# High and low parts of the stationary weight panels interleaved word by word in one tile, on a hybrid recurrent and attention step

## The chip, the cores and the metric

The kernel runs on one core of one Trainium2 chip, as one launch. The metric is device time in microseconds (us) from launch to end; lower is better. Durations of single instructions and waits are read from one profiled execution of the kernel before. Engines are named as the profile names them: PE (matrix multiplication), PEld (the loads of PE's stationary operand, which run beside PE's matmuls), DVE (vector engine), ACT (scalar engine), POOL (GpSimd), SP (issues most DMAs).

## The reference

One layer of a streaming encoder is computed for a prompt of 1024 rows and a sample of 64 rows, 1088 rows together, each 1024 wide, all in float32:

```
xn = rms_norm(x, g_pre)
z = xn @ w_in                                   # 1024 x 8208
xa, ga, q, k, v, gb, fl, ma, mb = split(z)      # branch A, branch B, merge gates
ua = causal_conv(xa);  ya = rg_lru(ua) * silu(ga)          # recurrence over the rows
yb = attention(q, k, v, cumsum(log_sigmoid(fl + b_f))) * silu(gb)   # 16 heads of 64
u = stack([ya, yb]) @ w_branch                   # two 1024 x 1024 products
mix = sum(sigmoid([ma, mb]) * u) @ w_o
h = x + rms_norm(mix, g_post)
h = h + rms_norm(sigmoid(h @ w_ple_gate) * (pe @ w_ple_proj), g_ple)
```

Keys, values, forget logarithms and the last states of the recurrence are outputs too. What the change touches are the products with `w_in` (all columns but those of v and the forget logits) and with `w_branch`.

## The kernel before, in words

**Three matmuls for one product.** Every float32 operand is split into a high part, which the ACT engine writes by a rounding copy (`copy_act`, line 83, output type fp32r), and a low part, which DVE writes as the difference of the value and its high part (`sub`, line 86). A product is then three matmuls that add into one PSUM bank: high by high, high by low, low by high (`three`, lines 163 to 166). Each matmul is preceded by its own load of the stationary operand, a block of 128 x 128 words. So there are as many loads as matmuls, 10117 of each.

**Panels.** In most of the kernel the stationary operand is a block of weights, and the activations, held transposed in SBUF as `xh`, `xl` (or `yah`, `yal`, `ybh`, `ybl`), stream past it. A panel is 128 columns of a weight matrix: 1024 x 128 words, kept as 8 blocks `wh[:, k, :]` (high) and 8 blocks `wl[:, k, :]` (low), each tile 128 partitions x 1024 words, in the pool `wpool` with two buffers per name. `load_panel` brings the raw words into `w_raw` by DMA; `split_next`, `book_split` or `weights_of`, by stage, has ACT and DVE split them; `panel_steps` (lines 185 to 195) or `dense` and `held` multiply: for each of three chunks of the 1088 rows (368, 368 and 352 of them) and each of 8 blocks k, three matmuls.

**Quads.** From about 147 to 413 us twelve pairs of panels go through a Strassen-like scheme (`split_pair` and `seven`, lines 626 to 925): seven products instead of eight, of half-size blocks, each over two half-banks of 272 rows. Weights for it are the raw halves (`a11`, `a12`, `a22`) and sums of them (`s1` to `s4`). `split` inside `split_pair` puts their high and low parts into `wpool` tiles of 8 blocks and into tiles `wh8`, `wl8` (8 blocks) and `wh4`, `wl4` (4 blocks) of a second pool. `product` (line 785) issues for each block and each of the three parts two matmuls of 272 rows (line 792), each with its own load.

**What sets the order.** PE's order is written out by hand. In the stages of attention and of the recurrence the orders of ACT and DVE are too, by planners with fixed costs; in the quads a scheduler orders ACT, DVE, POOL and SP by when operands and tiles come free. A tile is free for its next use when the last reader of its old content is done.

**Stages.** In order of time: values (v) and the transposition of x, 0 to 123 us, weights here being the moving operand; two panels; the quads; attention, with panels as fillers between its steps, 437 to 857 us; branch A with its recurrence, 857 to 1024; the product of ya, to 1119; of yb, to 1214; then `w_o` and the last gate, to the end, where weights are again the moving operand (`wqh`, `wql`).

**Where a high and a low part are not panels.** `wvh`, `wvl`, `wqh`, `wql`, `wph`, `wpl`, the gate blocks `g_h`, `g_l` of the recurrence, and one panel of the product of ya that is split into a free tile of `yb` (line 274's argument `rooms`) have tiles of their own.

Of the kernel before, what the change touches and what calls it, by code (L numbers as in the profile page):

```python
# [8 lines left out]
F32R = mybir.dt.float32r  # L9
# [4 lines left out]
P = 128  # L14
D = 1024
KT = D // P
# [50 lines left out]
def hybrid_step(tc, a, o):  # L67
# [4 lines left out]
    def sb(name, bufs=1, side=None):  # L72
        kw = {"side": side} if side else {}
        return Pool(tc, name=name, bufs=bufs, reuse_waits="tile", **kw)
# [4 lines left out]
    def f(ap):  # L79
        return ap.bitcast(F32)  # L80

    def copy_act(out, in_, scale=1.0):
        return act.activation(out=out, in_=in_, func=AF.Copy, scale=scale)  # L83

    def sub(eng, out, in0, in1):
        return eng.tensor_tensor(out=out, in0=in0, in1=in1, op=ALU.subtract)  # L86
# [121 lines left out]
    wpool = sb("wpool", bufs=2)  # L208
# [2 lines left out]
    raw_pair = w_raw.rearrange("p (k n) -> p k n", k=KT)  # L211
    raw_half = [w_raw[:, i * KT * P:(i + 1) * KT * P] for i in range(2)]

    def panels(src):
        return [src[..., i * P:(i + 1) * P] for i in range(2)]

# [32 lines left out]
    def look_ahead():  # L249

        while len(ahead) < 2:
            if held_back[0] and len(gates) <= n_gates - PLAIN // 2:
                return
            if not (gates or later):
                return
            src, tags = (gates or later)[0]
            if any(not e[3] and max(len(tags), e[4]) > 1 for e in ahead):
                return
            (gates or later).popleft()
            if len(tags) > 1:  # L260
                dst = raw_pair
                raws_ = panels(raw_pair)
            else:
                dst = raw_half[n_single[0] % 2].rearrange("p (k n) -> p k n", k=KT)
                raws_ = [dst]
                n_single[0] += 1
            load_panel(dst, src, tc.keep_in_program_order)
            for tag, raw in zip(tags, raws_):
                ahead.append([tag if isinstance(tag, tuple) else ("r", tag), raw, None, False, len(tags)])

    def split_next(eng, rooms=None):
        if ahead and ahead[0][2] is None:
            raw = ahead[0][1]
            wh, wl = rooms or [wpool.tile([P, KT, P], F32R, name=n) for n in ("wh", "wl")]
            copy_act(wh[:, :, :], raw)
            sub(eng, wl[:, :, :], raw, f(wh[:, :, :]))
            ahead[0][2:4] = (wh, wl), True

    def panel(eng=None):

        look_ahead()
        if not ahead:
            return None
        split_next(eng or dve)
        tag, _, w, *_ = ahead.popleft()
        look_ahead()
        split_next(eng or dve)
        look_ahead()
        return tag, w
# [152 lines left out]
    def weights(k, c):  # L442
        c0, w = VCH[c]
        return wvh[:, k, c0:c0 + w], wvl[:, k, c0:c0 + w]
# [51 lines left out]
    for name in ("conv_w", "conv_b", "b_rg_a", "b_rg_x", "a_param", "state_h", "state_conv"):  # L496
        n = a[name].shape[0]
# [76 lines left out]
    for b in range(2, NBLK + 1):  # L574
        _, n, t0 = x_src[b]
        for c, (_, w) in enumerate(VCH):
            acc = p1v.tile([P, 512], F32, name="vacc", tag="vacc")
            if b < NBLK:
                for k in range(KT):
                    turn_next(b, c, k)  # L580
                    wh, wl = weights(k, c)
# [24 lines left out]
        if b == NBLK - 2:  # L606
            look_ahead()
            split_next(dve)
        elif b == NBLK - 1:
            plain_1 = panel()  # L610
# [11 lines left out]
    def load_pair(i):  # L622
        raw = sp_.tile([P, KT, 2 * P], F32, name="wraw", tag="wraw", bufs=1)[:, :, :] if i % 2 else raw_pair
        src = quads[i][0]
        for dst, s in zip([raw] if len(src) == 1 else panels(raw), src):
            load_panel(dst, s)
        return panels(raw)

    def split_pair(i, raws_, got):

        a1, a2 = raws_
        a11, a12, a21, a22 = a1[:, :4, :], a1[:, 4:, :], a2[:, :4, :], a2[:, 4:, :]

        def split(pl, names, parts, bufs):
            n = 4 * len(names)
            sfx = "" if pl is wpool else str(n)
            wh = pl.tile([P, n, P], F32R, name="wh" + sfx, tag="wh" + sfx, bufs=bufs)
            wl = pl.tile([P, n, P], F32R, name="wl" + sfx, tag="wl" + sfx, bufs=bufs)
            for i_, x in enumerate(parts):
                ks_ = slice(4 * i_, 4 * i_ + x.shape[1])  # L640
                copy_act(wh[:, ks_, :], x)
                sub(dve, wl[:, ks_, :], x, f(wh[:, ks_, :]))
            for i_, name in enumerate(names):
                got[name] = wh[:, 4 * i_:4 * i_ + 4, :], wl[:, 4 * i_:4 * i_ + 4, :]

        s1, s2, s4 = (sp_.tile([P, 4, P], F32, name=f"s{j}")[:, :, :] for j in (1, 2, 4))
        pool.tensor_tensor(out=s1, in0=a21, in1=a22, op=ALU.add)
        sub(pool, s2, s1, a11)
        sub(pool, a21, a11, a21)
        sub(pool, s4, a12, s2)  # L650
        yield
        split(wpool, ("a11", "a12"), [a1[:, :, :]], 2)
        yield
        split(sp_, ("s2", "s3"), [s2, a21], 1)
        yield
        split(wpool, ("s1", "a22"), [s1, a22], 2)
        yield
        split(sp_, ("s4",), [s4], 1)
        yield
# [322 lines left out]
    def book(engine, at, ns, do=None):  # L982

        busy = booked[engine]
        while busy and busy[0][1] < now[0] - 20000.0:
            busy.pop(0)
        i = 0
        while i < len(busy) and busy[i][0] < at + ns:
            at = max(at, busy[i][1])
            i += 1  # L990
        busy.insert(i, (at, at + ns))
        if do is not None:
            serial[0] += 1
            heapq.heappush(agenda, (at, serial[0], do))
        return at + ns + HOP
# [23 lines left out]
    def book_split():  # L1019

        if ahead and ahead[0][2] is None:
            e = ahead[0]
            raw = e[1]
            wh = wpool.tile([P, KT, P], F32R, name="wh")
            wl = wpool.tile([P, KT, P], F32R, name="wl")
            e[2] = wh, wl

            def low():
                sub(dve, wl[:, :, :], raw, f(wh[:, :, :]))
                e[3] = True  # L1030
                look_ahead()

            at = book("A", now[0] + 5000.0, A_W, lambda: copy_act(wh[:, :, :], raw))
            book("D", at, D_W, low)
# [339 lines left out]
    def step(engine, ns, do, r=(), w=(), lag=0.0, after=(), table=None, bank=0, ahead_of=0.0, frees=False):  # L1374
        i = len(todo)
        deps = set(after)
        for x in (*r, *w):
            deps |= {written[x]} if x in written else set()
        for x in w:
            deps |= read_by.get(x, set())  # L1380
        for x in w:
            written[x], read_by[x] = i, set()
        for x in r:
            if x not in w:
                read_by.setdefault(x, set()).add(i)
        todo.append((engine, ns, do, deps, lag, table, bank, ahead_of, frees))
        return i
# [68 lines left out]
    def weights_of(tag, lag=0.0):  # L1456

        n = len(w_at)
        after = [last_use[n - 2]] if n > 1 else []
        if lag:  # L1460
            after.append(step("S", 0.0, lambda: None, after=w_at[-1:], lag=lag))
        got = {}

        def hi():
            look_ahead()
            e = next(x for x in ahead if x[0] == tag)
            got["e"] = e
            if e[2] is None:
                e[2] = tuple(wpool.tile([P, KT, P], F32R, name=x) for x in ("wh", "wl"))
                copy_act(e[2][0][:, :, :], e[1])  # L1470
                got["new"] = True

        def lo():
            e = got["e"]
            if "new" in got:
                sub(dve, e[2][1][:, :, :], e[1], f(e[2][0][:, :, :]))
            e[3] = True
            look_ahead()

        i = step("A", A_W if n else 0.0, hi, after=after)  # L1480
        w_at.append(step("D", D_W if n else 0.0, lo, after=[i]))

        def take():
            assert ahead[0][0] == tag
            got["w"] = ahead.popleft()[2]
            look_ahead()

        return got, take
# [349 lines left out]
    for of in range(KT):  # L1838
# [11 lines left out]
        else:  # L1850
            tag, w = panel()
# [42 lines left out]
    for of in range(KT):  # L1894
# [12 lines left out]
        tag, w = panel()  # L1907
# [77 lines left out]
    for q in range(NQ):  # L1985
# [7 lines left out]
        wh, wl = wo[q]  # L1993
        qc = slice(q * QW, (q + 1) * QW)
        for b in range(NBLK + 1):
            _, n, t0 = x_src[b]
# [97 lines left out]
    n = x_src[b][1]  # L2094
# [69 lines left out]
```

## Time and profile before

| | us |
|---|---|
| median of 3 runs (1456.34 to 1457.87) | 1456.99 |
| the profiled execution's own time | 1456.83 |
| its span, first to last instruction | 1454.9 |
| PE busy | 1438.2 |
| PEld busy | 1417.9 |
| DVE busy | 867.1 |
| ACT busy | 718.4 |
| POOL busy | 275.7 |

Between the span and the execution's own time lie 1.9 us. Matmuls are pipelined and their recorded durations overlap, so the pace of matmuls is read from the distance of their starts, not from their durations. The loads of the stationary operand overlap likewise.

### The profile page before, as it was taken

Reading aid. Unit: us, or ns where it says so; the run is one execution under the profiler, and the core shown is the slowest. Engines: PE = TensorE matmul, PEld = TensorE weight load, DVE = VectorE, ACT = ScalarE, POOL = GpSimd, SP = SyncE. Lnnn points to the kernel's source line nnn. Section 1 sums busy time; section 2 is a strip of 40 time slices with the busy share of each in tenths; the row PEclk is TensorE's granted clock in tenths of the full one; section 3 lists DMA queues with packets and bytes.
Section 4 is the critical chain, followed back from the end, with each engine's and each line's share of the span. In section 5 each row is a group of like instructions: output and inputs, shape, how many; then the busy total and the mean of one; then the engine's idle time right before and its main releaser. Section 6 shows DMA issues by size and latency. Waiting matters only on the chain.

```text
span 1454.9 us, 26374 instructions
## 1 busy us (share of the span) xinstructions
PE 1438.2 (99%) x10117; PEld 1417.9 (97%) x10117; DVE 867.1 (60%) x1571; ACT 718.4 (49%) x1389; POOL 275.7 (19%) x363
## 2 busy tenths in 40 slices
PE   8999999999999999999999999999999999999997
PEld 8999999999999999999999999999999999999997
DVE  5554765665425666666556557799745555248634
ACT  5424444443225666565555557869543333334633
POOL 0003333413222332333223210000122000000001
PEclk9999999999999999999999999999999999999999
DMA  5366455664276665636646242121486444214111
GB/s 206 114 137 99 143 161 179 176 186 120 82 215 160 118 148 146 139 105 158 103 114 159 51 100 51 51 58 33 162 294 212 153 150 137 74 46 146 51 45 44
DMA packets 140793, 182.85 MB, mean 126 GB/s; under 512 B 22788, under 2 KB 111404, under 8 KB 140668
## 3 DMA queue, kind: packets, MB, share of 16 engines
q1 hardware_dynamic: 122684, 154.90, 40.5%
q10 hardware_dynamic: 17680, 25.64, 5.0%
q8 instruction: 80, 1.31, 0.4%
q0 software_dynamic: 304, 0.62, 0.1%
q14 instruction: 45, 0.37, 0.1%
HBM read 122.65 MB, written 58.46 MB: 124 GB/s over the span
## 4 chain that ended last, share of the span: by engine, by line
PE 94%; DVE 2%; DMA 2%; ACT 1%; issue 1%; SPq 0%; ACTq 0%; DVEq 0%
PE quad L792 16%; PE acc L164 16%; PE acc L165 16%; PE acc L166 16%; PE tp L1145 4%; PE pv L1173 3%; PE pv L1175 3%; PE s L1123 2%; PE s L1124 2%; PE vacc L164 1%; PE vacc L166 1%; PE vacc L165 1%; PE vacc L457 1%; DMA out_v_prompt<-v_sb 1%; DMA wv_raw<-in_w_in 1%; PE tp L1953 1%
## 5 line engine op out<-in xcount | busy, mean ns | idle before, releaser
L164 PE MATMUL acc<-xh,wh 128*128 128x368 f32 (+1 forms) x768 | 252.7, 329 | 0.0
L165 PE MATMUL acc<-xl,wh 128*128 128x368 f32 (+1 forms) x768 | 251.5, 327 | 0.0
L166 PE MATMUL acc<-xh,wl 128*128 128x368 f32 (+1 forms) x768 | 251.0, 327 | 0.0
L164 PEld LDWEIGHTS acc<-xh,wh 128*128 128x128 f32 x768 | 144.6, 188 | 0.7
L165 PEld LDWEIGHTS acc<-xl,wh 128*128 128x128 f32 x768 | 144.7, 188 | 0.6
L166 PEld LDWEIGHTS acc<-xh,wl 128*128 128x128 f32 x768 | 144.7, 188 | 0.0
L1103 DVE CUSTOM_DVE_ANT_0 s<-s,mask 128x1024 f32<-128x1024 f32 (+7 forms) x128 | 95.5, 767 | 25.6 <-PE s L1124 25.3
L86 DVE TENSOR_TENSOR wl<-w_raw,wh 128x1024 fp32r<-128x1024 f32 (+1 forms) x65 | 74.7, 1149 | 60.4 <-ACT wh L83 55.4
L83 ACT ACTIVATE wh<-w_raw 128x1024 fp32r<-128x1024 f32 (+1 forms) x65 | 63.3, 975 | 76.1 <-PE acc L165 31.1
L1108 POOL TENSOR_SCALAR pb<-pb,sm 128x896 f32<-128x896 f32 (+1 forms) x64 | 61.6, 962 | 204.7 <-DVE sm L1107 183.9
L86 DVE TENSOR_TENSOR tl<-tp,th 128x512 fp32r<-128x512 f32 x96 | 65.8, 689 | 37.6 <-ACT th L83 37.5
L792 PE MATMUL quad<-xh,wh 128*128 128x272 f32 x384 | 80.7, 291 | 0.0
L792 PE MATMUL quad<-xl,wh 128*128 128x272 f32 x384 | 79.5, 288 | 0.0
L792 PE MATMUL quad<-xh,wl 128*128 128x272 f32 x384 | 79.4, 288 | 0.0
L1105 ACT ACTIVATE pb<-s,nm 128x896 f32<-128x896 f32 (+1 forms) x64 | 61.1, 954 | 33.3 <-DVE nm L1103 26.8
L83 ACT ACTIVATE th<-tp 128x512 fp32r<-128x512 f32 x96 | 56.9, 596 | 41.5 <-PE tp L1145 37.5
L164 PE MATMUL acc<-wqh,hth 128*128 128x256 f32 x256 | 72.8, 284 | 0.0
L164 PE MATMUL acc<-wqh,mxh 128*128 128x256 f32 x256 | 72.5, 283 | 0.0
L165 PE MATMUL acc<-wql,hth 128*128 128x256 f32 x256 | 72.2, 282 | 0.0
L166 PE MATMUL acc<-wqh,mxl 128*128 128x256 f32 x256 | 72.2, 282 | 0.0
L166 PE MATMUL acc<-wqh,htl 128*128 128x256 f32 x256 | 72.2, 282 | 0.0
L165 PE MATMUL acc<-wql,mxh 128*128 128x256 f32 x256 | 72.1, 282 | 0.0
(557 smaller groups left out, 4195.1 us busy)
## 6 DMA issues: line engine op xcount, KB each, us to landing
w_raw<-in_w_in SPq DMA_DIRECT2D x60, 256.0 KB
q<-d_q SPq DMA_DIRECT2D x48, 256.0 KB
k<-d_k SPq DMA_DIRECT2D x48, 256.0 KB
w_raw<-in_w_branch SPq DMA_DIRECT2D x32, 256.0 KB
w_raw<-in_w_in SPq DMA_DIRECT2D x56, 128.0 KB
wraw<-in_w_in SPq DMA_DIRECT2D x20, 256.0 KB
d_k<-oh ACTq DMA_DIRECT2D x16, 272.0 KB
d_k<-kl SPq DMA_DIRECT2D x16, 272.0 KB
```

Source lines behind the costliest of these rows:

```text
L83: return act.activation(out=out, in_=in_, func=AF.Copy, scale=scale)
L86: return eng.tensor_tensor(out=out, in0=in0, in1=in1, op=ALU.subtract)
L164: pe.matmul(out, ah, bh, start=start, stop=False)
L165: pe.matmul(out, ah, bl, start=False, stop=False)
L166: pe.matmul(out, al, bh, start=False, stop=stop)
L792: pe.matmul(acc[:, c, :CW], l[:, k, :], r[:, k, c * CW:(c + 1) * CW], start=(first and k == 0 and p == 0), stop=(k == 3 and p == 2), skip_ ...
L1103: at = book("D", now[0] + HOP_PE, per(D_MAX, n), lambda: dve.tensor_tensor_reduce(out=s[:, :n], in0=s[:, :n], in1=m, scale=-1.0, scalar=-N ...
L1105: free = book("A", at, per(A_EXP, n), lambda: act.activation(out=pr[:, :n], in_=s[:, :n], func=AF.Exp, scale=-1.0, bias=nm, accum_out=sm))
L1108: return free, book("G", at, per(G_NORM, n), lambda: pool.tensor_scalar(out=pr[:, :n], in0=pr[:, :n], scalar1=sm, scalar2=1.0, op0=ALU.mul ...
L1145: pe.transpose(tp[:, o0 + i * P:o0 + (i + 1) * P], pr[par][:, kb * P:(kb + 1) * P], ident[:, :])
L1173: pe.matmul(pv[:, :256], v, tl[:, c], start=(g == 0 and j == 0), stop=False)
L1175: tc.declare_no_dep(pe.matmul(pv[:, :256], v, th[:, c], start=False, stop=(g == q2 and j == 1)).ins, high.ins, reason="ordered through the ...
```

## The change

A new helper, `w_rooms`, allocates one tile of n blocks x 128 columns x 2 words in place of the two tiles of n blocks x 128 columns, and returns its even words as the high part and its odd words as the low part. All five places that allocated `wh` and `wl` for panels and quads use it. A room is as large as the two tiles it takes the place of (8 KB per partition for 8 blocks), with the same number of buffers. Nothing else in the code differs.

```diff
+    def w_rooms(n=KT, pl=wpool, name="w2", bufs=2):
+        t = pl.tile([P, n, P, 2], F32R, name=name, tag=name, bufs=bufs)
+        return t[:, :, :, 0], t[:, :, :, 1]
+
...
-            wh, wl = rooms or [wpool.tile([P, KT, P], F32R, name=n) for n in ("wh", "wl")]
+            wh, wl = rooms or w_rooms()
...
             n = 4 * len(names)
-            sfx = "" if pl is wpool else str(n)
-            wh = pl.tile([P, n, P], F32R, name="wh" + sfx, tag="wh" + sfx, bufs=bufs)
-            wl = pl.tile([P, n, P], F32R, name="wl" + sfx, tag="wl" + sfx, bufs=bufs)
+            wh, wl = w_rooms() if pl is wpool else w_rooms(n, pl, f"w2_{n}", bufs)
...
-            wh = wpool.tile([P, KT, P], F32R, name="wh")
-            wl = wpool.tile([P, KT, P], F32R, name="wl")
+            wh, wl = w_rooms()
...
-                e[2] = tuple(wpool.tile([P, KT, P], F32R, name=x) for x in ("wh", "wl"))
+                e[2] = w_rooms()
```

So three accesses change their step along the partition from one word to two: ACT's writes of the high parts, DVE's writes of the low parts (and its reads of the high parts), and PE's loads of the stationary operand. The number, kind, size and order of PE's matmuls are the same in both kernels, 10082 in the program's rows, and POOL's order is the same. Since high and low part are now one tile, a room is free only when the last reader of either part is done, and the scheduler of the quads places some copies differently.

On ACT in a quad that makes keys (`oh` goes to `d_k`), before; `wh<-wraw 128x1024` is the high part of `a11` and `a12` of the next pair, `ko<-quad` empties a PSUM bank:

```order
L83 ACTIVATE p__2186<-quad 128x544
L83 ACTIVATE wh<-wraw 128x1024
L83 ACTIVATE ko<-quad 128x544
L83 ACTIVATE oh<-ko 128x544
L836 DMA d_k<-oh 128x544
```

The same place of the changed kernel, where the room is called `w`:

```order
L83 ACTIVATE p__2172<-quad 128x544
L83 ACTIVATE ko<-quad 128x544
L83 ACTIVATE w_2241<-wraw 128x1024
L83 ACTIVATE oh<-ko 128x544
L838 DMA d_k<-oh 128x544
```

The copy that empties the bank now comes ahead of the copy of the weights.

On DVE in the quad behind it, which makes queries (`ko<-ko,oh` is their low part), before; `u` are sums read from PSUM, `cr` belongs to the running sums of the forget logarithms:

```order
L879 TENSOR_TENSOR u__2507<-quad,p__2467 128x544
L86 TENSOR_TENSOR wl<-w_raw,wh 128x1024
L86 TENSOR_TENSOR cr<-ct,cr 16x128
L741 TENSOR_SCALAR cr<-cr 16x256
L838 SCALAR_TENSOR_TENSOR ko<-ko,oh 128x544
L896 TENSOR_TENSOR u__2600<-quad,p__2467 128x544
```

The same place of the changed kernel:

```order
L881 TENSOR_TENSOR u__2489<-quad,p__2449 128x544
L86 TENSOR_TENSOR cr<-ct,cr 16x128
L743 TENSOR_SCALAR cr<-cr 16x256
L840 SCALAR_TENSOR_TENSOR ko<-ko,oh 128x544
L86 TENSOR_TENSOR w_2543<-w_raw,w_2543 128x1024
L898 TENSOR_TENSOR u__2581<-quad,p__2449 128x544
```

The low part of the next pair's weights moves behind three short instructions. These two moves recur in the other quads; outside the quads the orders of ACT and DVE are the same rows.

## The prediction

> **What bounds the kernel now.** I read the page's busy shares first, then the chain that ended last, then who waited for whom on PE, then a table by stage, and last single stretches of PE's timeline.
>
> ```profile
> PE 1438.2 (99%) x10117; PEld 1417.9 (97%) x10117; DVE 867.1 (60%) x1571; ACT 718.4 (49%) x1389; POOL 275.7 (19%) x363
> PE 94%; DVE 2%; DMA 2%; ACT 1%; issue 1%; SPq 0%; ACTq 0%; DVEq 0%
> PE quad L792 <- DVE u__1731 L896: 1.3, 1, 1.3
> ```
>
> PE is busy all the time, 94% of the chain runs through it, and in the quads it waited for another engine once, for 1.3 us. So nearly all of the time is the sum of the distances between matmul starts. By stage (columns: stretch, length, then busy time and count of PE, PEld, DVE, ACT, POOL):
>
> ```profile
> 147.00:413.00 266.00, 264.68 (x2118) 263.72 (x2118) 160.41 (x232) 103.67 (x188) 84.14 (x73) 1.00 0.53 155
> 857.00:1024.00 167.00, 167.00 (x1016) 167.00 (x1015) 135.15 (x139) 132.22 (x204) 10.22 (x28) 1.00 0.21 53
> ```
>
> The quads have ACT and DVE half free. The fullest stage beside PE is branch A, with DVE at 135 of 167 us. There PE still doesn't pause.
>
> **How many loads change.** The quads' line alone, from 123 to 1214 us, and the loads of the panels' low parts (one of three equal groups):
>
> ```profile
> 123.00:1214.00 1091.00, 259.92 (x2016) 254.62 (x2016) 1.00 0.50 133
> ...
> L166 PEld LDWEIGHTS acc<-xh,wl 128*128 128x128 f32 x768 | 144.7, 188 | 0.0
> L166 PEld LDWEIGHTS acc<-ybh,wl 128*128 128x128 f32 x192 | 36.2, 188 | 0.0
> L166 PEld LDWEIGHTS acc<-yah,wl 128*128 128x128 f32 x120 | 22.5, 188 | 0.0
> L166 PEld LDWEIGHTS held<-yah,wl 128*128 128x128 f32 x48 | 9.0, 188 | 0.0
> ```
>
> The quads have 2016 loads. The panels have 3 x (768 + 192 + 120 + 48) = 3384, of which two thirds, 2256, stand before matmuls of 368 columns and 1128 before matmuls of 352. So 5400 of 10117 loads are read in steps of two words.
>
> **What a load costs, and what hides it.** A load is recorded with 188 ns, but a matmul of 272 columns follows the last after less. The stretch of the quads in which PE had paused shows both numbers:
>
> ```profile
> 163.36 0.52 PE L792 MATMUL quad<-t4h,wh 128*128 128x272 f32 x2 [1.32 <-DVE u__1731 L896]
> 163.72 0.41 PE L792 MATMUL quad<-t4l,wh 128*128 128x272 f32 x2
> 163.97 0.41 PE L792 MATMUL quad<-t4h,wl 128*128 128x272 f32 x2
> ```
>
> Two pairs start 0.25 us apart, so the pace is 125 ns per matmul. The pair behind the pause took 0.52 us and not 0.41: its first load had no matmul to hide behind, and stood open with 0.11 us. The transposes of attention say the same. They are so narrow (128 columns) that their loads bind them:
>
> ```profile
> L1145 PE MATMUL tp<-ident,pb 128*128 128x128 f32 x416 | 64.0, 275 | 0.0
> ...
> 700.88 0.60 PE L1145 MATMUL tp<-ident,pb 128*128 128x128 f32 x4
> ```
>
> Four take 0.60 us, one takes 0.275, so three further ones cost 0.325 us, 108 ns each. I take 108 ns as the real length of a load with step one. The panels' pace comes from the starts of equal lines:
>
> ```profile
> 1201.61 0.32 PE L164 MATMUL acc<-ybh,wh 128*128 128x352 f32 x1
> ...
> 1202.10 0.33 PE L164 MATMUL acc<-ybh,wh 128*128 128x368 f32 x1
> ...
> 1202.60 0.32 PE L164 MATMUL acc<-ybh,wh 128*128 128x368 f32 x1
> ```
>
> Three matmuls of 352 columns took 0.49 us, 163 ns each; three of 368 took 0.50 us, 167 ns each. So a load is hidden with 125 - 108 = 17 ns to spare in the quads, and with 55 to 59 ns in the panels. This is the cover on which the forecast rests: the change costs nothing on PE while a load in steps of two words stays under 125 ns.
>
> By the Trainium skill, "TensorE: Matmul & The Clock Gate", section "LDWEIGHTS (loading the stationary operand)", the time of a load goes by its number of columns alone, P / 1.2 in ns, which is 107 ns for 128 columns; the 108 ns above agree. Nothing there speaks of a step.
>
> **The change, part by part.** *The loads in steps of two.* No row of before has a stationary operand with a step, so I bound it. Below: nothing is gained, since a load that is hidden already gives nothing back when it shortens, and a matmul streams its own 272 to 368 columns whatever the weights' step. Above: each word costs what two cost now, 2 x 108 = 216 ns for a load, as if the skipped words were read too. I take no change, 108 ns, because the nearest row is the load with step one itself: 128 words per partition in 108 ns, slower than the 272 words that the matmul beside it streams in 125, so that a load doesn't look limited by reading. Sum: 0 us; upper end worked out below.
>
> The Trainium skill has a rule that could speak against this: "SBUF — State Buffer", section "Specifications (TRN2)", says that the memory has lines of 16 bytes, that two hits per line are needed for full bandwidth, and that each cross to a new line pays. Steps of two words (8 bytes) leave exactly two hits per line: by the first half of the sentence the load stays at 107 ns and the sum at 0, by the second half it crosses twice as many lines. No run here shows a step, so it is a rival and has its price there.
>
> *ACT's and DVE's writes in steps of two.* The pieces concerned:
>
> ```profile
> L86 DVE TENSOR_TENSOR wl<-w_raw,wh x65: 678/1220/1780, 100.3 to 1191.5; 128x1024 fp32r<-128x1024 f32 x53, 128x512 fp32r<-128x512 f32 x12
> L83 ACT ACTIVATE wh<-w_raw 128x1024 fp32r<-128x1024 f32 (+1 forms) x65 | 63.3, 975 | 76.1 <-PE acc L165 31.1 <-PE quad L792 22.5 <-DMA out_v_prompt<-v_sb 11.2
> ```
>
> Both run near one word per ns (1024 words in 1220 and 975 ns), with type fp32r to and from SBUF. I take them as unchanged. At the upper end, twice as long, a piece gains 1.2 us on DVE and 1.0 on ACT. In the quads, with 160 and 104 of 266 us busy, that is hidden. In branch A it is 12 pieces, 12 x 1.22 = 14.6 us on DVE's 135 of 167: it still fits, but with 17 us to spare. Sum: 0; the end is 15 us if all of it came through.
>
> *One room instead of two tiles.* ACT's copy waits until the last reader of the low part, too, is done: in a quad's product the last two matmuls, 2 x 125 ns = 0.25 us more. The copy of the next pair's weights, its place and its first use:
>
> ```profile
> 202.98 1.06 ACT L83 ACTIVATE wh<-wraw 128x1024 fp32r<-128x1024 f32 x1 [5.13 <-PE quad L792]
> 203.95 0.60 ACT L83 ACTIVATE ko<-quad 128x544 f32<-128x544 f32 x1
> ...
> 204.08 1.23 DVE L86 TENSOR_TENSOR wl<-wraw,wh 128x1024 fp32r<-128x1024 f32 x1 [3.04 <-ACT wh L83]
> ...
> 215.69 0.50 PE L792 MATMUL quad<-xh,wh 128*128 128x272 f32 x2
> ```
>
> The low part is ready at 205.3 us and first read at 215.7, 10.4 us later. Moved behind the copy of 0.60 us on ACT, or behind three instructions on DVE, none longer than the pieces above, it is 1 to 3 us later and still 7 early. What waits behind the copy on ACT is `oh` and its DMA to `d_k`, read only in attention. The bank is emptied some 0.7 us sooner, but PE waited in the quads only once. POOL's and PE's orders stay. On SP some loads of raw panels trade places with stores; their cover is the same 10 us. Sum: 0, at most the 1.3 us of that one wait.
>
> **The sum** is the profiled execution's 1456.83 + 0, and that execution lies 0.16 under the median of 1456.99. I forecast 1456.9 us.
>
> **The rivals.** *A load takes twice as long* (slower, on PE, in all 5400 loads; decides as soon as a load needs over 125 ns in the quads, 163 in the panels). At 216 ns the loads set the pace: quads 2016 x (216 - 125) = 183 us, panels 2256 x (216 - 167) + 1128 x (216 - 163) = 111 + 60 us, together 354: 1811 us. For it: 97% of the span has a load under way, so nothing else could hide it. Against: a load reads one word at a time now. Chance 0.15.
>
> *A load takes half as long again*, 162 ns. Then only the quads pay, 2016 x (162 - 125) = 75 us: 1532 us. Chance 0.08.
>
> *A little slower elsewhere*: the written steps make the splits late in branch A (up to 15 us, half of it hidden, 7 us), or the scattered loads slow the streams beside them by 1 to 2 ns per matmul, 5400 x 1 to 2 ns = 5 to 11 us. 1460 to 1468 us, chance 0.11.
>
> *Faster*: the same contact between load and stream, with the other sign. From 272 to 368 columns the pace grows from 125 to 167 ns, 0.44 ns per column; 272 columns at 0.44 are 119 ns, so some 6 ns of each matmul don't go with its width. If part of that is the load's reading, other addresses could save 1 ns, 5.4 us: 1451 us, or 1.5 ns, 1449. Against: nothing in the rows ties those 6 ns to the addresses of the load. The Trainium skill, "TensorE: Matmul & The Clock Gate", Part 2, says that load and stream have read ports of their own, by which this and the slower twin could not happen; the trace can't tell. Chance 0.14.
>
> **How the numbers follow.** Forecast 0.52, with its own range 1454.0 to 1459.7 us, that is within 0.2%, about what a measurement of this kernel can tell from no change. Faster 0.14; slower 0.15 + 0.08 + 0.11 = 0.34. The range must leave out no more than 0.2: it leaves out the doubled load (0.15) and the tails, and reaches from 1448 to 1532, the load of one and a half.
>
> **What would show it.** Right: two pairs of the quads still 0.25 us apart, panels at 163 and 167 ns, and loads recorded with 188 ns. Wrong: a recorded load longer by about 54 or 108 ns, PEld's starts setting PE's, the quads' stretch longer than 266 us by 75 or 183. For the splits: mean times of the two pieces over 1.22 and 0.98 us, and waits of PE for them in branch A. The forecast falls with the first of these, since its cover in the quads is only 17 ns.

## The result, and the profile after

The changed kernel took 1462.32 us in the median of 6 runs (1461.69 to 1462.97), and the kernel before, run beside it on the same chip, 1456.96 (6 runs, 1456.34 to 1458.13). The ratio is 1.0033, with an interval of 1.0023 to 1.0043. It is 0.33% slower, more than the 0.2% that counted as no change. A second measurement on another chip gave 1463.07 (10 runs) against 1458.97 (20 runs): 1.0030, 1.0020 to 1.0039. Three executions of this study, of 2004.53, 2107.52 and 2857.19 us, stand far outside their series, whose other times lie within 6 us, and are left out of all counts of runs and all medians. The profiled execution took 1462.63 us, 5.8 us more than before, with a span of 1460.8 (before 1454.9).

The page of the changed kernel, busy shares, chain and three groups of panel loads (busy us and mean ns behind the bar; the new tile is called `w`):

```profile
PE 1443.1 (99%) x10117; PEld 1422.8 (97%) x10117; DVE 868.0 (59%) x1571; ACT 724.1 (50%) x1389; POOL 274.3 (19%) x363
PE 92%; DVE 3%; DMA 3%; ACT 1%; issue 1%; SPq 0%; ACTq 0%; DVEq 0%
L164 PEld LDWEIGHTS acc<-xh,w 128*128 128x128 f32 x768 | 149.9, 195 | 0.7
L165 PEld LDWEIGHTS acc<-xl,w 128*128 128x128 f32 x768 | 150.0, 195 | 0.5
L166 PEld LDWEIGHTS acc<-xh,w 128*128 128x128 f32 x768 | 149.7, 195 | 0.0
```

PE still bounds the kernel, with as many instructions. The recorded load grew from 188 to 195 ns, that is by 7 ns and not by the 54 or 108 ns of the two rivals with longer loads. The two stages that were tabulated before (the stretch of branch A is taken 5.6 us later now, since the stage begins 5.5 us later), and who was waited for in the quads:

```profile
147.00:413.00 266.00, 264.45 (x2092) 263.36 (x2092) 159.92 (x230) 105.90 (x188) 83.76 (x73) 1.00 0.52 152
862.60:1029.60 167.00, 167.00 (x1015) 167.00 (x1015) 135.17 (x139) 132.87 (x204) 10.25 (x28) 1.00 0.21 53
```

```profile
PE quad L794 <- DVE u__1724 L898: 1.3, 1, 1.3
```

In branch A, DVE (135.17 us) and ACT (132.87) are as busy as before, and PE has no gap. In the quads the one wait is still 1.3 us. Yet in the same 266 us of quads PE, busy throughout, started 2092 matmuls and not 2118. So each takes longer, and nobody is waited for longer than before.

One product of the quads, before and then with the change (start in us, length; equal neighbours are one row):

```profile
222.67 0.41 PE L792 MATMUL quad<-xl,wh 128*128 128x272 f32 x2
...
225.18 0.41 PE L792 MATMUL quad<-xh,wl 128*128 128x272 f32 x2
```

```profile
224.81 0.42 PE L794 MATMUL quad<-xl,w 128*128 128x272 f32 x2
...
227.38 0.42 PE L794 MATMUL quad<-xh,w 128*128 128x272 f32 x2
```

Between the two starts of each fence lie 20 matmuls: 2.51 us before, 125.5 ns each, and 2.57 us now, 128.5 ns each. This product, a12*B21, is the one that loses most (products are named by weights and activations, where B is a block of the activations and T a sum of blocks). Over the distances of starts within the quads' 84 products, without the 30 of over 200 ns that either kernel has, the mean went from 125.47 to 126.70 ns. All 1932 distances together are 244.98 us before and 247.54 now, 2.56 us more. The panels, in the product of yb, at the change of width:

```profile
1207.50 0.32 PE L164 MATMUL acc<-ybh,w 128*128 128x352 f32 x1
...
1207.98 0.33 PE L164 MATMUL acc<-ybh,w 128*128 128x368 f32 x1
...
1208.48 0.33 PE L164 MATMUL acc<-ybh,w 128*128 128x368 f32 x1
```

Three matmuls of 352 columns take 0.48 us (0.49 before), three of 368 take 0.50 as before. The trace's starts resolve it: 161.2 to 160.1 ns and 166.1 to 166.9 ns in this stage, which nearly cancel.

By stage, from starts of matmuls, the 5.9 us lie so:

| stage | before | change | difference |
|---|---|---|---|
| opening (no weights in steps) | 121.54 | 122.94 | +1.40 |
| quads | 265.82 | 268.86 | +3.04 |
| attention, with panels as fillers | 424.25 | 425.20 | +0.95 |
| branch A | 152.27 | 152.37 | +0.10 |
| product of ya | 95.24 | 95.41 | +0.17 |
| product of yb | 94.72 | 94.83 | +0.11 |
| `w_o` and the end | 233.15 | 233.15 | 0.00 |

The rest, 0.10, are the short panels between the stages. The opening and attention differ by up to 3.5 us between profiled executions also where nothing in them was changed (opening 121.5 to 125.1, attention 423.1 to 426.2 us over the 16 profiled executions of whole kernels in this study), so a difference of one pair of executions there says little. The pace of the fillers in attention says more: from 160.7 to 160.6 ns at 352 columns and from 167.2 to 168.0 ns at 368, which makes 0.4 us. Over all panels the paces make 0.8 us. The quads repeat better: 265.8 to 265.9 us in three executions of the code before, 268.6 to 268.9 in four of the change (two of the three and two of the four with another first tile, see below).

### The profile page after: what moved, and what is told of

It is laid out like the page before. It is cut to its first block, busy times and chain, and to the rows that moved or that the text cites. A ratio compares the mean times of both kernels' runs of the same rounds, so it can differ in the third digit from the quotient of the medians.

```text
span 1460.8 us, 26371 instructions
## 1 busy us (share of the span) xinstructions
PE 1443.1 (99%) x10117; PEld 1422.8 (97%) x10117; DVE 868.0 (59%) x1571; ACT 724.1 (50%) x1389; POOL 274.3 (19%) x363
## 4 chain that ended last, share of the span: by engine, by line
PE 92%; DVE 3%; DMA 3%; ACT 1%; issue 1%; SPq 0%; ACTq 0%; DVEq 0%
PE acc L164 16%; PE acc L166 16%; PE acc L165 16%; PE quad L794 16%; PE tp L1146 4%; PE pv L1174 3%; PE pv L1176 3%; PE s L1124 2%; PE s L1125 2%; DMA w_raw<-in_w_in 1%; PE vacc L461 1%; PE vacc L164 1%; PE vacc L165 1%; PE vacc L166 1%; DMA wv_raw<-in_w_in 1%; DMA q<-d_q 1%
## 5 line engine op out<-in xcount | busy, mean ns | idle before, releaser
L164 PE MATMUL acc<-xh,w 128*128 128x368 f32 (+1 forms) x768 | 253.5, 330 | 0.0
L166 PE MATMUL acc<-xh,w 128*128 128x368 f32 (+1 forms) x768 | 251.7, 328 | 0.0
L165 PE MATMUL acc<-xl,w 128*128 128x368 f32 (+1 forms) x768 | 251.6, 328 | 0.0
L164 PEld LDWEIGHTS acc<-xh,w 128*128 128x128 f32 x768 | 149.9, 195 | 0.7
L165 PEld LDWEIGHTS acc<-xl,w 128*128 128x128 f32 x768 | 150.0, 195 | 0.5
L166 PEld LDWEIGHTS acc<-xh,w 128*128 128x128 f32 x768 | 149.7, 195 | 0.0
L794 PE MATMUL quad<-xh,w 128*128 128x272 f32 x768 | 137.0, 291 | 0.0
L794 PEld LDWEIGHTS quad<-xh,w 128*128 128x128 f32 x768 | 113.4, 195 | 0.2
L86 DVE TENSOR_TENSOR w<-w_raw,w 128x1024 fp32r<-128x1024 f32 (+1 forms) x65 | 73.9, 1137 | 54.8 <-ACT w L83 50.0
L83 ACT ACTIVATE w<-w_raw 128x1024 fp32r<-128x1024 f32 (+1 forms) x65 | 68.6, 1057 | 49.1 <-PE acc L166 30.1
L794 PE MATMUL quad<-xl,w 128*128 128x272 f32 x384 | 80.2, 290 | 0.0
```

Source lines behind the costliest of these rows:

```text
L164: pe.matmul(out, ah, bh, start=start, stop=False)
L165: pe.matmul(out, ah, bl, start=False, stop=False)
L166: pe.matmul(out, al, bh, start=False, stop=stop)
L794: pe.matmul(acc[:, c, :CW], l[:, k, :], r[:, k, c * CW:(c + 1) * CW], start=(first and k == 0 and p == 0), stop=(k == 3 and p == 2), skip_ ...
```

## The experiments

Three causes were held against each other. **A**: the loads in steps of two words. **B**: one room for two tiles, with its moved copies. **C**: ACT's and DVE's writes in steps of two. Within A it was open how a load that should be hidden costs anything; the expectations call the ways **A1** and **A2** and say each time what they mean. Besides times, one row carries most readings: the quads' loads before matmuls of `xh`, with their recorded ns (least/median/most) and the starts of the first and the last, whose distance is the length of the quads. Before:

```profile
L792 PEld LDWEIGHTS quad<-xh,wh x384: 186/188/192, 146.7 to 412.0; 128*128 128x128 f32 x192
L792 PEld LDWEIGHTS quad<-xh,wl x384: 187/188/192, 147.2 to 412.5; 128*128 128x128 f32 x192
```

From 146.7 to 412.5 are 265.8 us at 188 ns a load. With the change:

```profile
L794 PEld LDWEIGHTS quad<-xh,w x768: 193/195/199, 148.1 to 417.0; 128*128 128x128 f32 x192
```

268.9 us at 195 ns.

### The room alone, with halves in place of words

```diff
-        t = pl.tile([P, n, P, 2], F32R, name=name, tag=name, bufs=bufs)
-        return t[:, :, :, 0], t[:, :, :, 1]
+        t = pl.tile([P, 2 * n, P], F32R, name=name, tag=name, bufs=bufs)
+        return t[:, :n, :], t[:, n:, :]
```

> One room for high and low part as in the change, same order of all engines as the change, but the high part fills the first half of the room and the low part the second, so no access has a step of two. Theory A (the step costs): back to the kernel before, 1457.0 us, within 0.7. Theory B (one room, later release and other order in the quads cost): as the change, 1462.3 us. Theory C (ACT's longer writes cost): as before, 1457.0.

1458.94 us (11 runs) against 1458.28 (29 runs), ratio 1.0009, 1.0001 to 1.0018. The quads' row:

```profile
L794 PEld LDWEIGHTS quad<-xh,w x768: 186/188/192, 150.2 to 416.3; 128*128 128x128 f32 x192
```

266.1 us at 188 ns, with the pace at 125.49. Room and orders are those of the change, and the quads don't lose. Since the interval ends just above 1, it was measured again beside the change:

> The room of the change with high and low part as halves of it, as a control on the same chip. Theory A: 3.5 us under the change, and within 0.7 us of the kernel before. Theory B: as the change.

1458.39 us (11 runs) against 1458.97, ratio 0.9996, 0.9987 to 1.0005. Its quads took 266.8 us, but at a pace of 125.48: within the products both kernels with halves take 245.03 and 245.02 us (before 244.98). What is more lies between the products, 21.1 and 21.8 us in all, and that scatters in kernels of the code before too (20.5 to 21.1 us over five). So room and moves cost nothing that the whole times show, and in the quads at most 0.9 us, which scatter may explain: B falls as the cause.

### Words in the quads alone, words in the panels alone

```diff
-            wh, wl = w_rooms() if pl is wpool else w_rooms(n, pl, f"w2_{n}", bufs)
+            wh, wl = w_rooms(words=True) if pl is wpool else w_rooms(n, pl, f"w2_{n}", bufs, True)
```

Here `w_rooms` makes halves unless `words` is set. In the other kernel it makes words unless the quads ask for halves.

> One room everywhere; word by word in the quads' weights only, halves in the panels. Theory A: the quads' part of the loss, 2016 matmuls at 1.5 ns, 3 us: 1460.0 us, the quads' stretch 269 us and all behind it as before. Theory B: 1462.3 us. Theory C: about 1457, since ACT has half its time free in the quads.

> One room everywhere; word by word in the panels only, halves in the quads' weights. Theory A: chunks of 368 columns lose 0.8 ns per matmul and chunks of 352 win 1.1, so the panels nearly cancel; what is left is what attention lost, 1 to 2 us: 1458.5 us. Theory B: 1462.3 us. Theory C: most of the loss, 1460 to 1462, since ACT is fullest in attention and branch A.

With words in the quads 1460.81 us (11 runs), ratio 1.0020, 1.0011 to 1.0028; in the panels 1460.04 (12 runs), 1.0012, 1.0004 to 1.0021; both against 1458.28. The quads' rows, of the first and of the second:

```profile
L797 PEld LDWEIGHTS quad<-xh,w x768: 193/195/199, 148.1 to 416.7; 128*128 128x128 f32 x192
```

```profile
L797 PEld LDWEIGHTS quad<-xh,w x768: 186/188/192, 147.6 to 413.9; 128*128 128x128 f32 x192
```

268.6 us at 195 ns, and 266.3 us at 188 ns; within the products 247.58 and 245.00 us. The quads' loss is there exactly when their weights are in steps. The expectations count from 1457.0 us; from this chip's 1458.28 the quads lost 2.5 us (A had 3.0, B 5.3, C none) and the panels 1.8 (A had 1.5, B 5.3, C 3 to 5). The panels' 1.8 us have an interval of 0.6 to 3.1 us; the stages of branch A, ya and yb hold only 0.4 of it (152.37, 95.40 and 94.83 us). The paces of all panels, which are those of the change, hold 0.8, half of it in attention (423.40 us long, no longer than before). The two parts together, 2.5 and 1.8, make 4.3 us, about the whole.

That ACT's writes grew is seen in their forms (busy us and mean ns behind the bar), before and after:

```profile
L86 DVE TENSOR_TENSOR wl<-w_raw,wh 128x1024 fp32r<-128x1024 f32 x53 | 65.3, 1233 | 60.4 <-ACT wh L83 55.4 <-DMA w_raw<-in_w_in 2.9 <-PE gacc L166 1.4
L83 ACT ACTIVATE wh<-w_raw 128x1024 fp32r<-128x1024 f32 x53 | 55.9, 1056 | 76.1 <-PE acc L165 31.1 <-PE quad L792 22.5 <-DMA out_v_prompt<-v_sb 11.2
```

```profile
L86 DVE TENSOR_TENSOR w<-w_raw,w 128x1024 fp32r<-128x1024 f32 x53 | 65.6, 1237 | 54.8 <-ACT w L83 50.0 <-DMA w_raw<-in_w_in 3.7 <-DMA q<-d_q 0.6
L83 ACT ACTIVATE w<-w_raw 128x1024 fp32r<-128x1024 f32 x53 | 60.5, 1144 | 48.9 <-PE acc L166 30.1 <-DMA out_v_prompt<-v_sb 11.3 <-PE held L166 2.7
```

ACT's copy of 1024 words went from 1056 to 1144 ns, DVE's difference stayed at 1233 and 1237. The one wait of PE in the quads is as long as before, and in branch A PE has no gap: C is real on ACT, and hidden. Nor is it the writes that slow PE's stream. In the quads' distances during which neither engine wrote weights the mean went from 125.36 to 126.81 ns (1132 and 1117 of them). That is no less than in those that a write covered to nine tenths or more (125.62 to 126.59, 681 and 672 of them).

### What a load costs, by its step

A kernel of nothing but trains of loads and matmuls, at steps of 1, 2, 3, 4 and 8 words, and ACT's and DVE's writes with the same steps.

```diff
+    def one(s):
+        def get(part, k):
...
+            at = k * P * s + part
+            return rooms[:, at:at + P * s - s + 1:s]
+        return get
...
+                pe.matmul(out[:, 0, :n], w(wp, k), x[:, k, t0:t0 + n], start=(k == 0 and p == 0), stop=(k == ks - 1 and p == 2))
```

> This kernel computes nothing of the reference: it runs only trains of matmuls with the stationary operand read in steps of 1, 2, 3, 4 and 8 words, ahead of moving operands of 64, 128, 272, 352 and 368 columns (the moving operands laid out as in the quads and panels), with no other engine at work, and then high and low parts of 1024 words written by ACT and DVE in those steps. Theory A (the load itself is read more slowly in steps of two, and this reaches the matmuls where the cover is thin): at 64 and 128 columns, where the loads set the pace, step two takes 115 ns against 108 for step one, and at 272 columns about 1.5 ns more per matmul; steps of four and eight, with one word in each line of 16 bytes, take up to 216 ns. Theory B (order and release of the room): step one and step two have the same pace to 0.3 ns at all widths. ACT: step two 1144 ns against 1056; DVE the same for both.

Between matmuls of 64 columns, where only the loads set the pace, they followed each other after 112, 118, 174, 233 and 238 ns in the median, at full clock. The granted clock, the share of full clock that PE was given, was 0.78 over this run, full in some stretches and half in others; at half clock the distances at steps one to three were 213 ns, and the trains of 128 columns, all at half clock, tell nothing. At full clock 272 columns went from 125.9 and 126.3 ns at step one to 125.4 and 125.8 at step two, so the expected 1.5 ns did not come, while 352 went from 158.4 to 160.1 and 368 from 168.9 to 170.1. Since all trains of a width had one name there, a second kernel named them by step, with trains of 512 columns between them:

> Computes nothing of the reference: trains of matmuls again, with the weights in steps of one, two, three and four words, each train behind a train of 512 columns with step one, so that the clock stays full. At 64 columns, where loads set the pace: 112, 118, 174 and 233 ns, as the first look found. Theory A1 (a load is a whole: it costs only where it outlasts the stream): at 272 columns step two has the pace of step one, and the 1.4 ns of the quads came from elsewhere. Theory A2 (the load's reading also gets in the way of the stream beside it): step two costs 1 to 2 ns per matmul at 272, 352, 368 and 512 columns alike, however much cover there is. At 512 columns steps three and four (174 and 233 ns) should cost 0 to 10 ns by A1 and clearly more by A2.

Its narrow trains on PE's timeline (the last word of the name is the step; from row to row of a step there are three matmuls):

```profile
40.73 0.28 PE L106 MATMUL narrow_one<-xl,rooms 128*128 128x64 f32 x1
...
41.07 0.28 PE L106 MATMUL narrow_one<-xl,rooms 128*128 128x64 f32 x1
```

```profile
152.76 0.28 PE L106 MATMUL narrow_two<-xl,rooms 128*128 128x64 f32 x1
...
153.11 0.28 PE L106 MATMUL narrow_two<-xl,rooms 128*128 128x64 f32 x1
```

```profile
265.59 0.34 PE L106 MATMUL narrow_three<-xl,rooms 128*128 128x64 f32 x1
...
266.11 0.34 PE L106 MATMUL narrow_three<-xl,rooms 128*128 128x64 f32 x1
```

```profile
393.75 0.39 PE L106 MATMUL narrow_four<-xl,rooms 128*128 128x64 f32 x1
...
394.45 0.40 PE L106 MATMUL narrow_four<-xl,rooms 128*128 128x64 f32 x1
```

0.34, 0.35, 0.52 and 0.70 us for three, all at full clock; over whole trains, without their first distance, 111.6, 117.6, 173 and 233 ns each. So a load in steps of two is 6 ns longer: still under the quads' 125. By cover alone the change would have cost nothing there. But the same kernel's trains of 512 columns, the widest and best covered (matmuls before `xh`: first and last start behind the colon):

```profile
L106 PE MATMUL wide_one<-xh,rooms x64: 389/389/393, 103.1 to 124.6; 128*128 128x512 f32 x64
L106 PE MATMUL wide_two<-xh,rooms x64: 392/394/394, 215.3 to 237.5; 128*128 128x512 f32 x64
L106 PE MATMUL wide_three<-xh,rooms x64: 393/396/407, 338.0 to 360.4; 128*128 128x512 f32 x64
L106 PE MATMUL wide_four<-xh,rooms x64: 398/402/463, 484.3 to 506.8; 128*128 128x512 f32 x64
```

96 matmuls of `xh` and `xl` have 95 distances between these starts: 21.5 us at step one, 226 ns each, and 22.2 us at step two, 234 ns. The trace's starts give 226.8 and 233.3. Above loads of 118 ns, matmuls of 227 ns followed each other 6.5 ns later, so here a load that ends long before the matmul does wasn't free. At steps three and four they took 235.6 and 237.3 ns, 8.8 and 10.5 more than at step one: about the 0 to 10 ns of A1, not clearly more, as A2 had it. At the other widths step two changed little, in both directions: 256 columns 119.9 to 120.0, 272 columns 126.5 to 125.6, 352 columns 158.4 to 160.0, 368 columns 166.8 to 166.7. So A2's 1 to 2 ns at all widths alike is out, and a charge per matmul that goes by the step alone with it. Each train had one place of its operands; what of these differences is the place's, the trains can't tell.

### Steps of four in the quads

```diff
-            return t[:, :, :, 0], t[:, :, :, 1]
+            t = t.rearrange("p k n -> p (k n)").rearrange("p (a n c) -> p a n c", c=4, n=P)
...
+        k = self.k0 + key[1]
+        return self.t[:, k // 2, :, self.part + 2 * (k % 2)]
```

The weights of the quads lie as high, low, high, low of two blocks, so that each load reads every fourth word.

> One room everywhere; in the quads high and low parts of two blocks share a room, so that each is read and written in steps of four words, halves in the panels. Theory A: a load then takes 233 ns and outlasts the stream; the quads' pace goes from 126 to 233 ns, 2016 x 107 ns = 216 us, the quads' stretch about 482 us, 1675 us in all. Theory B (order and room): about as the change, 1462 us.

```profile
L815 PEld LDWEIGHTS quad<-xh,w x768: 307/330/338, 148.7 to 630.7; 128*128 128x128 f32 x192
```

1675.17 us, and 482.0 us of quads at 330 ns a load. The stretch grew by 216 us, 2016 loads at 107 ns, which is 125.5 to 233 ns. This is the mechanism of the rival with the doubled load, at 233 ns a load where it had 216, and it comes with the fourth word, not with the second.

By the Trainium skill, "SBUF — State Buffer", section "Specifications (TRN2)", a line of 16 bytes has to be hit twice for full bandwidth, and each new line has its price. That fits these loads: the step of two keeps two hits a line and costs 5%, and from two to four words the load goes by the lines that it touches (64, 96 and 128 for 128 words, 1.8 ns each as an estimate from the three times).

### Where the weights and the moving operand lie

The loss in the quads differs by product: 2.7 ns for a12*B21, none for s4*B22 (means of the distances of starts under 200 ns; the expectations, from a slightly different choice of distances, have 2.9, 0.1 and for all products 1.3 to 1.4 ns). To see whether the place matters, a small tile ahead of all others was doubled or left out. The first expectation is that of the change as it is, measured again.

```diff
-    cst.tile([P, 8], F32, name="lead")
+    cst.tile([P, 16], F32, name="lead")
```

> The change itself, beside the next kernel on the same chip. Theory A: 3.0 us over the halves kernel in the quads and 0.5 us in the panels, 3.5 us in all; opening and attention differ from run to run by 1 to 2 us either way without reason in the change. Theory B: as the halves kernel, within 0.7 us.

> The kernel before without that tile, all 32 bytes back. Theories as for the longer one: A2 another pace than 125.5 ns in some products, A1 the same pace.

> The kernel before with the unused tile at the start of SBUF 16 words long instead of 8, so that nearly all tiles lie 32 bytes further on. Theory A2 (what a load takes from the stream beside it depends on where the two read): the pace of the quads, 125.5 ns, moves by some tenths of a ns to 2 ns, differently for the seven products, and the time by up to 5 us either way. Theory A1 (only the load's own length counts): the pace stays at 125.5 within 0.1 and the time at that of before.

> The change without the first tile. A2: another loss than 1.3 ns, product by product. A1: 126.8 ns as in the change.

> The change with the first tile 16 words long. A2: the loss of 1.3 ns per matmul in the quads changes in size or sign with the addresses, product by product. A1: 126.8 ns as in the change, since the load of 118 ns is the same.

The change as it is lay 4.7 us over the halves kernel (1463.07 and 1458.39), where A had 3.5. With the other first tiles, none and doubled, the quads' pace stayed at 125.46 and 125.47 before, and 126.72 and 126.71 with the change: no effect, where A2 expected one. The tile moves the weights and the moving operands of the quads together, so nothing between the two had changed, and the runs tell less than was meant. Stages with one operand in a pool at the other end did move: `w_o` took 98.55 us with no such tile, 99.96 with the doubled one, and 100.74 as it is, in both kernels. By whole times (against 1458.97 for the first, 1458.65 in 24 runs for the others): the change again 1.0030, before without the tile 0.9988 (0.9978 to 0.9998) and doubled 1.0001 (0.9991 to 1.0011), the change without it 1.0016 (1.0006 to 1.0025) and doubled 1.0040 (1.0025 to 1.0055, 4 runs only). Median against median, the change is 0.2 to 0.4% behind the kernel before at each of the three places.

So a second pair of places moves the moving operands by 32 and by 64 bytes, through an unused tile in their pool. By the order in which the kernel opens its pools this isn't all that moves, as the expectations have it: the weights s2, s3 and s4 lie in a pool behind and move along. Against their moving operands only a11, a12, s1, a22 and the panels of `w_in` changed their place.

```diff
+    xpool.tile([P, 8], F32, name="xlead")
```

> The kernel before, with an unused tile of 8 words put ahead of the tiles that hold xh, xl and the combinations of input and product panels, so that all moving operands lie 32 bytes further on against the weights; nothing else changes. Theory A2 (what the stream pays beside a load depends on where the two lie against each other): the pace in the quads' products moves away from 125.5 ns by over 0.3 ns, product by product, and the quads' stretch from 265.8 us by over 0.6 us. Theory A1 (what the stream pays depends on the step of the load alone): 125.5 ns and 265.8 us as before. Either way the whole stays within 1455 to 1460 us.

> The same with an unused tile of 16 words, 64 bytes. Theory A2: the quads' pace moves away from 125.5 ns by over 0.3 ns, and not as with 8 words. Theory A1: 125.5 ns and 265.8 us.

> The changed kernel with the unused tile of 8 words ahead of the moving operands. Theory A2: the quads' pace moves away from 126.8 ns, the products that paid 2.9 ns (a12*B21) and 0.1 ns (s4*B22) change places or sizes; the quads' stretch moves from 268.6 us by over 0.6 us. Theory A1: 126.8 ns and 268.6 us, and the products as in the change.

> The changed kernel with the unused tile of 16 words. Theory A2: the quads' pace moves away from 126.8 ns, and not as with 8 words. Theory A1: 126.8 ns and 268.6 us.

Single runs of 1461.04, 1458.67, 1464.06 and 1463.51 us, beside one of 1457.12 of the kernel before; the first lies outside the 1455 to 1460 us that both theories had. Means over the distances of starts under 200 ns within the quads' products, in ns, with two products by name, and the length of the quads in us:

| place of the moving operands | pace before | pace change | a12*B21, change | s4*B22, change | quads before | quads change |
|---|---|---|---|---|---|---|
| as it is | 125.47 | 126.70 | 127.75 | 126.47 | 265.82 | 268.86 |
| 32 bytes on | 125.70 | 126.53 | 126.50 | 126.64 | 265.93 | 268.09 |
| 64 bytes on | 125.31 | 126.44 | 126.84 | 125.61 | 265.80 | 268.25 |

The product of the fences above, in the two kernels of 64 bytes, before and change:

```profile
223.49 0.41 PE L793 MATMUL quad<-xl,wh 128*128 128x272 f32 x2
...
225.99 0.42 PE L793 MATMUL quad<-xh,wl 128*128 128x272 f32 x2
```

```profile
224.19 0.41 PE L795 MATMUL quad<-xl,w 128*128 128x272 f32 x2
...
226.72 0.42 PE L795 MATMUL quad<-xh,w 128*128 128x272 f32 x2
```

2.50 us for 20 matmuls before, 2.53 with the change: 1.5 ns lost on each, where it was 3 ns at the old place. Neither theory has it whole. The length of the quads moved by at most 0.8 us with the place, and the loss is there at all three places, 0.8 to 1.2 ns per matmul, 2.2 to 3.0 us in all (A1, that it belongs to the step). By product, at the three places, a12*B21, where the place changed, lost 2.7, 0.9 and 1.6 ns (A2), and s2*T2 and s3*T3, whose weights moved along, lost 1.0 to 1.1 ns at each. But the weights of s4*B22 moved along too, and it lost 0.0, 0.7 and -0.5 ns. So what a product pays does vary with the place, but the place of its two operands against each other isn't all that decides it.

## Why the prediction was wrong

The measured 1462.3 us lies outside the 1454.0 to 1459.7 us that stood for no change, the forecast. That it lies within the wide range is no merit: the range reaches to 1532 us for a load of 162 ns, which didn't come.

- **What bounds the kernel** was right. PE has no new wait, and all that changed is the distance of matmul starts.
- **The count**, 2016 quad loads and 3384 in panels, stands, but the two groups don't pay alike.
- **The real length of a load**, 108 ns from two readings of the trace, was 111.6 where the loads alone set the pace. In steps of two it is 117.6. The value taken, no change, was off by 6 ns, and the end of 216 ns is near what a step of four costs (233).
- **The step that failed** is "the change costs nothing on PE while a load in steps of two words stays under 125 ns". The load stays under 125, and the quads still lost 0.8 to 1.2 ns per matmul. The working took cover for all that binds load and stream. The trains of 512 columns show how far cover can fail, at their one place: 109 ns of cover, and 6.5 ns lost. The term for the loads, put at 0, measured by the paces 1.8 to 2.6 us in the quads, by place, and 0.8 to 2.2 us in the panels, 3.3 to 4.5 us together (2.6 and 0.8 with all tiles as they are).
- **The bounds of the load**, nothing gained and 216 ns, held for its length. What they left out was a loss beneath full cover. That stood among the rivals, as "a little slower elsewhere", at 1 to 2 ns per matmul on all 5400: the mechanism that came, by size nearest in the quads (1.2 ns at the place as it is), too high for the panels, where at that place 352 columns gained about what 368 lost. Over all 5400 loads the paces make 0.6 to 0.8 ns each.
- **ACT's and DVE's writes**: 0 on the path, as forecast, though ACT's are 8% longer, 88 ns for 12 copies in branch A or 1.1 us, all hidden. The 975 ns that the prediction read for 1024 words is a mean with the 12 shorter copies in it; by form it was 1056 ns.
- **One room, moved copies**: 0, as forecast, within a microsecond; the room with halves shows it.
- **The rival "faster, by the same contact"** wasn't seen in the quads as a whole at any of three places. Its reason, that some ns of a matmul don't go with its width and may hang on addresses, was sound: at the place as it is, paces of 352 columns did fall by a nanosecond.

What stays open: by the whole time the change costs 3.0 to 6.2 us at its five places (5.4 and 4.1 as it is), and the paces of quads and panels, the fillers of attention among them, hold 3.3 to 4.5 of them. Where the rest lies isn't shown; the opening and attention scatter by 3 us between executions of kernels of either kind. And by what path a load slows the matmul beside it isn't shown, only that it depends on the load's step, and that its size varies with the width and the place of the tiles.

In the Trainium skill, "TensorE: Matmul & The Clock Gate", Part 2, load and stream have a read port of their own each. The slower stream above a covered load, 125.5 to 126.7 ns in the quads and 226.8 to 233.3 ns in the trains, doesn't agree with two ports that share nothing behind them.

## What to carry to other kernels

Work beneath a longer instruction isn't free because it ends sooner: price the contact as well as the cover, and where thousands of instructions have it, 1 ns of each can already be above the noise of a measurement, as the quads' 2.5 us in 1458 were. Keep a stationary operand in steps of one word where it costs nothing, and never in steps of three or four where matmuls are narrower than 174 or 233 ns. Before an effect of a nanosecond per instruction is put down to an edit, move the operands by some bytes and see how much of it stays.

## What the runs showed of the hardware

- A load of 128 columns took 112, 118, 174, 233 and 238 ns at steps of 1, 2, 3, 4 and 8 words: 58 to 59 ns times the step from two to four, and nearly flat behind it.
- ACT's and DVE's writes of four times 1024 words took, by step of 1, 2, 3, 4 and 8, ACT 4.34, 4.56, 6.30, 8.09 and 8.22 us, DVE 5.00, 5.01, 6.21, 8.00 and 8.11. The first two and the last of ACT, and DVE at step four:

```profile
509.93 4.34 ACT L134 ACTIVATE rooms<-raw 128x1024 fp32r<-128x1024 f32 x4 [489.79 <-PE c_s L106]
519.39 4.56 ACT L134 ACTIVATE rooms<-raw 128x1024 fp32r<-128x1024 f32 x4 [5.13 <-DVE rooms L136]
...
557.93 8.22 ACT L134 ACTIVATE rooms<-raw 128x1024 fp32r<-128x1024 f32 x4 [8.12 <-DVE rooms L136]
```

```profile
549.85 8.00 DVE L136 TENSOR_TENSOR rooms<-raw 128x1024 fp32r<-128x1024 f32 x4 [8.21 <-ACT rooms L134]
```

- The place of operands alone moved the pace of equal matmuls by up to 2.6 ns: in the kernel before, panels of 368 columns in branch A ran at 166.3 ns, and at 168.9 and 167.5 with the moving operands 32 and 64 bytes on. The place isn't all: with the doubled first tile the first panel of the product of yb ran at 170.1 ns and the seven behind it at 166.1, though their weights alternate between the same two tiles. Several paces of the trains lay on a grid of 6.7 ns (120, 160, 166.7, 173.3, 226.7, 233.3).
